# Transposing v on VectorE in 32x32 blocks, with stores to DRAM that put the blocks in place

## The chip, the core and the metric

One core of one Trainium2 chip runs the whole kernel. The metric is device time in microseconds of one execution; the median of several executions is compared between two kernels. The engines are TensorE (PE, its weight loads are shown apart as PEld), VectorE (DVE), ScalarE (ACT), GpSimd (POOL) and SyncE (SP), which issues nearly all transfers. The transfers of SP run on 16 DMA engines that all its transfers share.

## What is computed

Two layers of a small trunk over 640 tokens (128 context tokens and 512 latent ones) of width 1024. Layer A is a chunked gMLP mixer. Layer B is a bidirectional gated DeltaNet with 8 heads, and the change lies in it. Cut to what matters, per head:

```python
proj = h @ w_in                                   # k, q (128 wide), v, z (256 wide) per head
qkv = silu(short_conv(qkv, conv_w))               # 5 taps along the tokens
q, k = l2norm(q) * D_K ** -0.5, l2norm(k)
# gated delta rule, forward and backward over the tokens, state S of 128 x 256:
# S_t = exp(g_t) (I - beta_t k_t k_t^T) S_{t-1} + beta_t k_t v_t^T ;  o_t = S_t^T q_t
o = o_f + flip(o_b)
y = (o * rsqrt(mean(o * o) + eps) * norm_g) * silu(z)
```

The projections leave k, q and v with the channels on the partitions and the tokens along the free dimension. The scan needs v with the tokens on the partitions, so v has to be transposed.

## The kernel before, in words

Layer B is one long software pipeline over the heads. A window `w` is the time of one head: in window `w` the four projections of head `w + 2` are made (`project_head`: k, q and the two halves of v, called q = 0, 1, 2, 3 in the code), the chunk matrices of head `w + 1` (`chunk`), the scan of head `w` (`scan`) and the norm and gate of head `w - 1` (`norm_o`, `gate_z`). `stages()` gives each part a start and an end in units of windows and `PIECES` says into how many pieces its generator is cut; `turns()` sorts all pieces by time. The order of the instructions of PE and SP is the order of these pieces, written down at build time. VectorE, ScalarE and GpSimd get theirs from a scheduler that simulates the program.

After a projection comes `conv` (ScalarE the first tap, L845, VectorE the other four, L848, then Tanh on ScalarE, L851, and `(tanh + 1) * acc` on VectorE, L853). That yields twice the silu, in a buffer `cacc` of 128 channels by 642 columns. For the two halves of v, `post_v` follows (L934): `flip` (L240) transposes the five 128x128 blocks on TensorE into the PSUM tile `px`, of which there is one: four blocks together (tokens 128 to 639), then the first one alone. ScalarE copies each of the two results to the buffer `nat` and halves it there (L938), and one transfer stores `nat` to the DRAM tensor `kvd` of the head (L941). `nat` has one buffer, which k's `post_k` (L905, L907) and both halves of v use in turn. One window later `chunk` loads k from `kvd` (L961), and the scan loads v from it, 128 tokens by 256 columns at a time (`load`, L1097, four buffers). VectorE makes `r` from that v and PSUM (L1115), and TensorE multiplies `r` with the chunk matrices (L1125, L1126).

Of the kernel before, what the change touches and what calls it, by code (L numbers as in the profile page):

```python
# [6 lines left out]
F32 = mybir.dt.float32  # L7
F32R = mybir.dt.float32r
F16 = mybir.dt.float16
AF = mybir.ActivationFunctionType  # L10
# [3 lines left out]
P = 128  # L14
# [9 lines left out]
H = 8  # L24
# [23 lines left out]
NORM_LEN = 1.0  # L48
CONV_AT, CONV_LEN, POST_AT, POST_LEN, NORM_AT, GATE_AT, GATE_STEP = 1.0, 1.0, 2.0, 1.0, 0.4, 1.5, 0.6
CAT, CLEN = 0.0, 0.9  # L50
CSTEP = CLEN / 40 * 4
# [22 lines left out]
def tok(c):  # L74
# [7 lines left out]
PIECES = {"scan": 24, "chunk": 40, "norm_o": 4, "gate_z": 4, "conv": 8, "post_k": 13,  # L82
          "post_q": 7, "post_v": 5, "gates": 7, "gates_e": 26, "residual": 17}


def stages():
# [5 lines left out]
    for w in range(-2, H + 1):  # L92
# [11 lines left out]
        for i, (kind, h, q) in enumerate(slots):  # L104
            i = start + i * wide
            add("project_" + kind, (h, q), i / n, (i + wide) / n, 17)
            if kind == "head":
                i += wide - 1
                add("conv", (h, q), (i + CONV_AT) / n, (i + CONV_AT + CONV_LEN) / n)
                add(("post_k", "post_q", "post_v", "post_v")[q], (h, q), (i + POST_AT) / n,  # L110
                    (i + POST_AT + (KLEN if q == 0 else POST_LEN)) / n)
        if w == -2:
# [95 lines left out]
class Trunk:  # L208
# [421 lines left out]
    def layer_b(self):  # L630
# [4 lines left out]
        self.e_d = self.dram([P, TT, H, P], "ed")  # L635
        self.kv_d = [self.dram([P, TT, P + DV], "kvd") for _ in range(H)]
        with contextlib.ExitStack() as banks, pool("b_c") as bc:
# [11 lines left out]
            self.convw = t(bc, [P, H, 4, CONV], F32, "convw")  # L649
            nc.sync.dma_start(self.convw, a["convw"])  # L650
            self.ngT = t(bc, [P, 2], F32, "ngT")
            nc.sync.dma_start(self.ngT, a["ngT"])
# [185 lines left out]
    def conv(self, h, q):  # L838

        nc, t = self.nc, self.t  # L840
        xp = self.acc[h, q]
        acc = t(self.b2, [P, PADN], F32, "cacc")
        self.acc[h, q] = acc, xp
        w = self.convw[:, h, q]
        nc.scalar.activation(acc, xp[:, 0:PADN], AF.Copy, scale=w[:, 0:1])  # L845
        yield
        for i in range(1, CONV):
            nc.vector.scalar_tensor_tensor(acc, xp[:, i : i + PADN], w[:, i : i + 1], acc, op0=ALU.mult, op1=ALU.add)  # L848
            yield
        th = xp[:, 2 : 2 + PADN]  # L850
        nc.scalar.activation(th, acc, AF.Tanh, scale=0.5)  # L851
        yield
        nc.vector.scalar_tensor_tensor(acc, th, 1.0, acc, op0=ALU.add, op1=ALU.mult)  # L853
        if q != 1:
            self.gap(xp)
        yield
# [29 lines left out]
    def post_k(self, h, q):  # L886
# [7 lines left out]
        for c0 in (1, 0):  # L894
# [11 lines left out]
            yield  # L906
        nc.sync.dma_start(self.kv_d[h][:, :, 0:P], kn)  # L907
        for c0 in (1, 0):
# [22 lines left out]
    def post_v(self, h, q):  # L931
        nc, t = self.nc, self.t
        s, _ = self.acc[h, q]
        v = t(self.b1, [P, TT, P], F32, "nat")  # L934
        for c0 in (1, 0):
            p = self.flip(lambda c: s[:, tok(c)], c0)
            yield
            nc.scalar.mul(v[:, c0 : c0 + p.shape[1], :], p, 0.5)  # L938
            if c0:
                yield  # L940
        nc.sync.dma_start(self.kv_d[h][:, :, P * (q - 1) : P * q], v)  # L941
        yield

    def chunk(self, h, cs):
# [15 lines left out]
        kn = t(b1, [P, nt, P], F32, f"kn{nt}")  # L960
        nc.sync.dma_start(kn, self.kv_d[h][:, those, 0:P])  # L961
        pg = bank()
# [116 lines left out]
    def scan(self, h):  # L1079
# [15 lines left out]
        def load(c):  # L1095
            v = t(b1, [P, DV], F32, "v", bufs=KVB)
            nc.sync.dma_start(v, self.kv_d[h][:, c, P : P + DV])  # L1097
            return v
# [322 lines left out]
```

## Time and profile before

| | |
|---|---|
| median of 3 runs | 1356.4 us (1355.96 to 1357.52) |
| the profiled execution: its time | 1356.03 us |
| the profiled execution: its span | 1354.2 us |
| TensorE busy | 1282.5 us (95%) |
| VectorE busy | 875.7 us (65%) |
| ScalarE busy | 578.7 us (43%) |
| GpSimd busy | 502.0 us (37%) |
| DMA, queue of SP | 157.0 MB, 35.3% of 16 engines' span |

The span runs from the first to the last instruction; the execution's own time is 1.8 us longer. Busy shares are means over stages. Layer B's pipeline runs from about 554 us to 1238 us. Busy time of TensorE counts each matmul from its start to its modelled end, and matmuls overlap.

### The profile page before, as it was taken

Reading aid. Unit: us, or ns where it says so; the run is one execution under the profiler, and the core shown is the slowest. Engines: PE = TensorE matmul, PEld = TensorE weight load, DVE = VectorE, ACT = ScalarE, POOL = GpSimd, SP = SyncE. Lnnn points to the kernel's source line nnn. Section 1 sums busy time; section 2 is a strip of 40 time slices with the busy share of each in tenths; the row PEclk is TensorE's granted clock in tenths of the full one; section 3 lists DMA queues with packets and bytes.
Section 4 is the critical chain, followed back from the end, with each engine's and each line's share of the span. In section 5 each row is a group of like instructions: output and inputs, shape, how many; then the busy total and the mean of one; then the engine's idle time right before and its main releaser. Section 6 shows DMA issues by size and latency. Waiting matters only on the chain. (4 is left out here: it accounts for less than half of the span.)

```text
span 1354.2 us, 22812 instructions
## 1 busy us (share of the span) xinstructions
PE 1282.5 (95%) x8773; PEld 1137.3 (84%) x8773; DVE 875.7 (65%) x1655; ACT 578.7 (43%) x1352; POOL 502.0 (37%) x503
## 2 busy tenths in 40 slices
PE   7999999999999999888999999999999999999996
PEld 4688999999997887778888898999899898887785
DVE  4654744444447566798677778686787868656357
ACT  2333522222224334665545354564545546443320
POOL 0221422222223434354343536355464646520024
PEclk9999999999999999998999999999999999999999
DMA  8512233333336324142122422234233242445732
GB/s 337 168 63 93 94 125 125 125 125 125 125 125 218 118 76 145 56 140 86 50 77 73 136 78 65 100 89 153 79 125 108 85 139 88 133 141 174 261 117 78
DMA packets 90254, 163.17 MB, mean 120 GB/s; under 512 B 9089, under 2 KB 55457, under 8 KB 90017
## 3 DMA queue, kind: packets, MB, share of 16 engines
q1 hardware_dynamic: 88704, 156.99, 35.3%
q10 hardware_dynamic: 1440, 4.72, 1.0%
q8 instruction: 69, 1.13, 0.3%
q14 instruction: 41, 0.33, 0.1%
HBM read 135.97 MB, written 25.71 MB: 119 GB/s over the span
## 5 line engine op out<-in xcount | busy, mean ns | idle before, releaser
L231 POOL TENSOR_TENSOR wlo<-wraw,whi 128x256 fp32r<-128x256 f32 (+1 forms) x188 | 194.4, 1054 | 261.6 <-ACT whi L230 261.6
L235 PE MATMUL pp<-hThi,whi 128*128 128x320 f32 (+1 forms) x784 | 280.1, 357 | 0.2 <-ACT hThi L230 0.2
L237 PE MATMUL pp<-hTlo,whi 128*128 128x320 f32 (+1 forms) x784 | 244.7, 312 | 0.4 <-POOL hTlo L231 0.4
L236 PE MATMUL pp<-hThi,wlo 128*128 128x320 f32 (+1 forms) x784 | 244.1, 311 | 0.0
L230 ACT CAST whi<-wraw 128x256 fp32r<-128x256 f32 (+1 forms) x262 | 143.5, 593 | 84.6 <-PE pacc L236 57.6
L235 PE MATMUL pacc<-hThi,whi 128*128 128x320 f32 x512 | 159.6, 312 | 0.0
L237 PE MATMUL pacc<-hTlo,whi 128*128 128x320 f32 x512 | 158.3, 309 | 0.0
L236 PE MATMUL pacc<-hThi,wlo 128*128 128x320 f32 x512 | 158.2, 309 | 0.0
L848 DVE SCALAR_TENSOR_TENSOR cacc<-xp,convw,cacc 128x642 f32<-128x642 f32 x128 | 137.7, 1076 | 25.0 <-ACT cacc L845 23.6
L235 PEld LDWEIGHTS pp<-hThi,whi 128*128 128x128 f32 (+1 forms) x784 | 148.8, 190 | 3.9 <-ACT hThi L230 0.3
L236 PEld LDWEIGHTS pp<-hThi,wlo 128*128 128x128 f32 (+1 forms) x784 | 148.6, 190 | 4.0
L237 PEld LDWEIGHTS pp<-hTlo,whi 128*128 128x128 f32 (+1 forms) x784 | 147.7, 188 | 1.8 <-POOL hTlo L231 0.7
L231 DVE TENSOR_TENSOR wlo<-wraw,whi 128x1024 fp32r<-128x1024 f32 (+1 forms) x74 | 87.7, 1196 | 60.0 <-ACT whi L230 59.5
L248 POOL TENSOR_TENSOR rs<-ve,mhalf 128x1 f32<-128x1 f32 (+2 forms) x39 | 40.1, 1028 | 170.1 <-DVE ve L246 166.7
L235 PEld LDWEIGHTS pacc<-hThi,whi 128*128 128x128 f32 x512 | 96.1, 188 | 3.1 <-issue 2.2
L236 PEld LDWEIGHTS pacc<-hThi,wlo 128*128 128x128 f32 x512 | 96.1, 188 | 0.0
L237 PEld LDWEIGHTS pacc<-hTlo,whi 128*128 128x128 f32 x512 | 96.1, 188 | 0.0
L256 POOL TENSOR_SCALAR gsq<-gsq 128x320 f32<-128x320 f32 (+1 forms) x52 | 27.7, 532 | 138.4 <-ACT gsq L255 137.4
L257 DVE TENSOR_TENSOR gsq<-pacc,gsq 128x320 f32<-128x320 f32 (+1 forms) x52 | 29.1, 565 | 73.9 <-POOL gsq L256 73.8
L255 ACT ACTIVATE gsq<-pacc 128x320 f32<-128x320 f32 (+1 forms) x52 | 25.7, 498 | 106.2 <-PE pacc L237 102.3
L235 PE MATMUL pacc<-whi,hThi 128*128 128x512 f32 x160 | 63.1, 406 | 7.6 <-ACT whi L230 4.4
L1032 ACT CAST TU<-pt 128x512 f16<-128x512 f32 (+1 forms) x120 | 57.2, 525 | 26.4 <-PE pt L1029 25.5
(333 smaller groups left out, 2974.9 us busy)
## 6 DMA issues: line engine op xcount, KB each, us to landing
wraw<-in_w_b SPq DMA_DIRECT2D x48, 512.0 KB
wraw<-in_w_ada SPq DMA_DIRECT2D x37, 512.0 KB
wraw<-in_w_uz SPq DMA_DIRECT2D x32, 512.0 KB
v<-kvd SPq DMA_DIRECT2D x72, 128.0 KB
wraw<-in_a_wo SPq DMA_DIRECT2D x16, 512.0 KB
wraw<-in_b_wo SPq DMA_DIRECT2D x16, 512.0 KB
kvd<-nat SPq DMA_DIRECT2D x24, 320.0 KB
cacc<-yd SPq DMA_DIRECT2D x24, 320.0 KB
```

Of the source, the lines that this page charges most:

```text
L230: self.nc.scalar.copy(hi, src)
L231: (e_lo or self.nc.vector).tensor_tensor(lo, src, f32(hi), op=ALU.subtract)
L235: mm(out, l_hi, r_hi, start=start, stop=False)
L236: mm(out, l_lo, r_hi, start=False, stop=False)
L237: mm(out, l_hi, r_lo, start=False, stop=stop)
L248: nc.gpsimd.tensor_tensor(r, ve, self.mhalf[:, 0:n], op=ALU.pow)
L255: nc.scalar.activation(sq, u, AF.Square)
L256: nc.gpsimd.tensor_scalar(sq, sq, GB, 1.0, op0=ALU.mult, op1=ALU.add)
L257: nc.vector.tensor_tensor(sq, u, sq, op=ALU.mult)
L848: nc.vector.scalar_tensor_tensor(acc, xp[:, i : i + PADN], w[:, i : i + 1], acc, op0=ALU.mult, op1=ALU.add)
L1032: nc.scalar.copy(part, p.rearrange("p s k t (j b) -> p s (k t j) b", b=b))
```

## The change

v is no longer transposed by TensorE. VectorE transposes `cacc` in blocks of 32x32 (two instructions for each half of v, one of 128x512 and one of 128x128), straight from SBUF to the buffer `nat`. Such an instruction transposes each 32x32 block where it stands. What is left, that block row `b` of channels belongs in column block `b` of the result, is done by four stores, one for each group of 32 partitions, each of 32x20 runs of 32 numbers (128 bytes). For that `kvd` becomes a plain matrix with a row for each token. The halving goes into the weights of v's convolution: they are multiplied by 0.5 once, on GpSimd, and Tanh of v takes its input as it is. Five empty pieces stand between the transposes and the stores, and `post_v` has 7 pieces over 1.4 units in place of 5 over 1.0.

```diff
+VLEN = 1.4
-          "post_q": 7, "post_v": 5, "gates": 7, "gates_e": 26, "residual": 17}
+          "post_q": 7, "post_v": 7, "gates": 7, "gates_e": 26, "residual": 17}
-                    (i + POST_AT + (KLEN if q == 0 else POST_LEN)) / n)
+                    (i + POST_AT + (KLEN, POST_LEN, VLEN, VLEN)[q]) / n)
-        self.kv_d = [self.dram([P, TT, P + DV], "kvd") for _ in range(H)]
+        self.kv_d = [self.dram([NT, P + DV], "kvd") for _ in range(H)]
+            nc.gpsimd.tensor_scalar(self.convw[:, :, 2:4], self.convw[:, :, 2:4], 0.5, 0.0, op0=ALU.mult, op1=ALU.add)
-        nc.scalar.activation(th, acc, AF.Tanh, scale=0.5)
+        nc.scalar.activation(th, acc, AF.Tanh, scale=0.5 if q < 2 else 1.0)
-        nc.sync.dma_start(self.kv_d[h][:, :, 0:P], kn)
+        nc.sync.dma_start(self.kv_d[h].rearrange("(c p) n -> p c n", p=P)[:, :, 0:P], kn)
-        v = t(self.b1, [P, TT, P], F32, "nat")
-        for c0 in (1, 0):
-            p = self.flip(lambda c: s[:, tok(c)], c0)
-            yield
-            nc.scalar.mul(v[:, c0 : c0 + p.shape[1], :], p, 0.5)
-            if c0:
-                yield
-        nc.sync.dma_start(self.kv_d[h][:, :, P * (q - 1) : P * q], v)
+        v = t(self.b1, [P, NT], F32, "nat")
+        nc.vector.transpose(v[:, P:NT], s[:, tok(1).start : tok(4).stop])
+        yield
+        nc.vector.transpose(v[:, 0:P], s[:, tok(0)])
+        for _ in range(5):
+            yield
+        rows = self.kv_d[h].rearrange("(a i) n -> i a n", i=32)
+        for b in range(4):
+            at = P * (q - 1) + 32 * b
+            nc.sync.dma_start(rows[:, :, at : at + 32],
+                              v[32 * b : 32 * b + 32].rearrange("p (a n) -> p a n", n=32))
         yield
-            nc.sync.dma_start(v, self.kv_d[h][:, c, P : P + DV])
+            nc.sync.dma_start(v, self.kv_d[h][c * P : (c + 1) * P, P : P + DV])
```

The loads of k in `chunk` take the same rows from the new layout. Three places where the order moves, all in the window of the fifth head, which stands at 880 to 955 us in the trace of before. The line numbers of the changed kernel are up to 7 higher.

SP, from the end of that head's first half of v to its second half and the loads of v for the scan of the head before (`kvd_4838` is the fifth head's tensor, `kvd_4837` the fourth's; `wraw` is a block of weights, `x` and `rn` belong to the residual, `yd` to the gate). Before:

```order
L961 DMA kn_1803_9808<-kvd_4838 128x2x128
L701 DMA x_80_498<-rn_9675 128x256
L696 DMA rn_9890<-n_76_494 128x256
L941 DMA kvd_4838<-nat_9784 640x1x128
L1215 DMA yd_4821<-z_1502_8471 128x640
L166 DMA wraw_9965<-in_w_b 128x1024
L701 DMA x_81_499<-rn_9890 128x256
L1097 DMA v_10025<-kvd_4837 128x256
L1097 DMA v_10027<-kvd_4837 128x256
```

and now:

```order
L968 DMA kn_1784_9765<-kvd_4838 128x2x128
L704 DMA x_80_498<-rn_9638 128x256
L947 DMA kvd_4838<-nat_9560 32x20x32 x4
L699 DMA rn_9849<-n_76_494 128x256
L1222 DMA yd_4821<-z_1490_8448 128x640
L167 DMA wraw_9922<-in_w_b 128x1024
L704 DMA x_81_499<-rn_9849 128x256
L947 DMA kvd_4838<-nat_9745 32x20x32 x4
L1104 DMA v_9986<-kvd_4837 128x256
L1104 DMA v_9988<-kvd_4837 128x256
```

The second half's one store stood ahead of the gate's store and the weights; its four stores now stand behind them, right ahead of two loads of v. The first half's stores have moved behind the last load of k.

VectorE, where the second half of v is now transposed, and the first use of those loads (L1115, now L1122). Before:

```order
L1213 SCALAR_TENSOR_TENSOR z_1502_8471<-px_9913,ngT_4869,z_1502_8471 128x128
L1134 SCALAR_TENSOR_TENSOR S_9978<-S_9597,scal_4871,ps_9936 128x256
L1140 TENSOR_TENSOR o_9794<-o_9794,ps_9936 128x256
...
L1213 SCALAR_TENSOR_TENSOR z_1552_8666<-px_10012,ngT_4869,z_1552_8666 128x128
L1115 SCALAR_TENSOR_TENSOR r_10079<-ps_10030,neg_4872,v_10025 128x256
L1115 SCALAR_TENSOR_TENSOR r_10082<-ps_10034,neg_4872,v_10027 128x256
L1022 TENSOR_TENSOR Y_1864_10121<-pt_10100,wm_4861 128x2x4x16
```

and now:

```order
L1220 SCALAR_TENSOR_TENSOR z_1490_8448<-px_9872,ngT_4870,z_1490_8448 128x128
L1141 SCALAR_TENSOR_TENSOR S_9935<-S_9562,scal_4872,ps_9893 128x256
L939 STREAM_TRANSPOSE nat_9745<-cacc_9549 128x512
L941 STREAM_TRANSPOSE nat_9745<-cacc_9549 128x128
L1147 TENSOR_TENSOR o_9751<-o_9751,ps_9893 128x256
...
L1220 SCALAR_TENSOR_TENSOR z_1538_8635<-px_9969,ngT_4870,z_1538_8635 128x128
L1029 TENSOR_TENSOR Y_1844_10082<-pt_10061,wm_4861 128x2x4x16
...
L1122 SCALAR_TENSOR_TENSOR r_10040<-ps_9991,neg_4873,v_9986 128x256
L1122 SCALAR_TENSOR_TENSOR r_10043<-ps_9995,neg_4873,v_9988 128x256
```

The two transposes stand between the state update `S` and the output `o`, and the two `r` have moved behind three products `Y` of the chunk part.

VectorE earlier in the same window, at the output `o` of the scan's first unit. Before:

```order
L859 MEMSET xp_766_4887 128x2
L982 SCALAR_TENSOR_TENSOR M_1781_9721<-pe_1779_9714,beta_4873,masks_4857 128x128 x3
L1140 TENSOR_TENSOR o_9603<-o_9603,ps_9696 128x256
L982 SCALAR_TENSOR_TENSOR M_1781_9721<-pe_1779_9714,beta_4873,masks_4857 128x128
L1004 TENSOR_TENSOR TU_1787_9753<-pt_9754,wm_756_4859 128x2x128
```

and now:

```order
L862 MEMSET xp_766_4888 128x2
L989 SCALAR_TENSOR_TENSOR M_1763_9682<-pe_1761_9675,beta_4874,masks_4857 128x128 x2
L1147 TENSOR_TENSOR o_9568<-o_9568,ps_9659 128x256
L989 SCALAR_TENSOR_TENSOR M_1763_9682<-pe_1761_9675,beta_4874,masks_4857 128x128 x2
L1011 TENSOR_TENSOR TU_1769_9714<-pt_9715,wm_756_4859 128x2x128
```

`o` has moved ahead of one of the four masked products `M`.

## Rows read from the trace of the kernel before

**Rows 1.** Page, part 1: busy us (share of the span) and instructions
```profile
PE 1282.5 (95%) x8773; PEld 1137.3 (84%) x8773; DVE 875.7 (65%) x1655; ACT 578.7 (43%) x1352; POOL 502.0 (37%) x503
```

**Rows 2.** Windows: stretch, length, busy PE PEld DVE ACT POOL (x), PEclk, DMA share, GB/s
```profile
554.00:1165.00 611.00, 577.33 (x4498) 533.81 (x4497) 472.94 (x971) 326.59 (x925) 304.06 (x328) 0.99 0.32 99
...
880.00:955.00 75.00, 73.01 (x585) 68.12 (x583) 57.97 (x122) 39.32 (x112) 41.70 (x48) 1.00 0.38 116
...
602.00:609.00 7.00, 4.65 (x31) 4.08 (x29) 7.00 (x13) 1.11 (x3) 4.52 (x5) 1.00 0.38 122
609.00:617.00 8.00, 5.27 (x23) 4.52 (x24) 7.65 (x15) 2.15 (x4) 5.04 (x5) 0.59 0.01 4
```

**Rows 3.** Tiles px and nat: count, duration ns min/median/max, first and last start, forms
```profile
L240 PE MATMUL px<-ident,cacc x120: 270/272/474, 575.3 to 1160.4; 128*128 128x128 f32 x120
...
L938 ACT ACTIVATE nat<-px x32: 257/438/602, 598.6 to 1160.9; 128x512 f32<-128x512 f32 x16, 128x128 f32<-128x128 f32 x16
```

**Rows 4.** Timeline of PE around two flips: start, us, instruction [idle before, releaser]
```profile
913.63 0.31 PE L237 MATMUL pp<-hTlo,whi 128*128 128x320 f32 x1
913.78 0.60 PE L240 MATMUL px<-ident,cacc 128*128 128x128 f32 x4
914.21 1.03 PE L1112 MATMUL ps<-S,kq 128*128 128x256 f32 x4
915.95 1.13 PE L1112 MATMUL ps<-S,kq 128*128 128x256 f32 x4 [0.71 <-DVE o L1140]
...
920.84 0.31 PE L237 MATMUL pp<-hTlo,whi 128*128 128x320 f32 x1
920.99 0.27 PE L240 MATMUL px<-ident,cacc 128*128 128x128 f32 x1
...
921.25 0.31 PE L236 MATMUL pp<-hThi,wlo 128*128 128x320 f32 x1
```

**Rows 5.** Timeline of PE in the first two heads: flips of v that waited, and what followed
```profile
609.13 0.66 PE L240 MATMUL px<-ident,cacc 128*128 128x128 f32 x4 [2.49 <-DVE cacc L853]
...
614.18 0.26 PE L1017 MATMUL pt<-TU,A 128*128 128x64 f16 x2 [2.60 <-DVE TU L1004]
...
679.15 1.11 PE L240 MATMUL px<-ident,cacc 128*128 128x128 f32 x4 [4.44 <-DVE cacc L853]
```

**Rows 6.** Timeline of DVE: idle behind the places where the transposes are put
```profile
898.27 0.69 DVE L1059 TENSOR_TENSOR R<-R,pt 128x512 f16<-128x512 f16 x1 [1.55 <-PE pt L1057]
...
926.00 0.48 DVE L1134 SCALAR_TENSOR_TENSOR S<-S,scal,ps 128x256 f32<-128x256 f32 x1 [1.56 <-PE ps L1126]
```

**Rows 7.** Groups of DVE by form, SBUF to SBUF: count, busy us, mean ns, idle before
```profile
L1052 DVE TENSOR_TENSOR R<-id,T 128x512 f16<-128x512 f16 x16 | 8.6, 538 | 3.7 <-ACT T L1050 3.5
...
L351 DVE TENSOR_TENSOR vh<-vh,y 128x512 f32<-128x512 f32 x8 | 6.9, 878 | 0.0
...
L353 DVE TENSOR_SCALAR vh<-vh,st 128x128 f32<-128x128 f32 x8 | 2.8, 344 | 0.2
```

**Rows 8.** Windows around three transfers that ran alone: kvd store, rn load, abrow load
```profile
843.00:845.50 2.50, 2.50 (x25) 2.40 (x24) 1.63 (x4) 0.00 (x0) 1.66 (x2) 1.00 0.46 131
...
543.50:545.25 1.75, 1.75 (x14) 1.23 (x11) 0.75 (x3) 1.48 (x4) 0.58 (x1) 1.00 0.04 6
918.00:919.50 1.50, 1.50 (x11) 1.45 (x10) 1.35 (x5) 0.75 (x2) 1.39 (x3) 1.00 0.28 87
```

**Rows 9.** Timeline of SP's queue, fifth head: start, us to issue
```profile
910.11 0.54 SPq L941 DMA_DIRECT2D kvd<-nat  x1
...
913.91 0.46 SPq L701 DMA_DIRECT2D x<-rn  x1
...
925.83 0.94 SPq L1097 DMA_DIRECT2D v<-kvd  x2
```

**Rows 10.** Timelines of DVE and PE: where the loaded v is used
```profile
932.40 0.48 DVE L1115 SCALAR_TENSOR_TENSOR r<-ps,neg,v 128x256 f32<-128x256 f32 x1 [0.83 <-PE ps L1112]
...
940.02 0.59 PE L1125 MATMUL ps<-r,G 128*128 128x256 f32 x2
```

More of the change, by code (lines that the diff above doesn't have):

```diff
@@ L960, in chunk @@
         kn = t(b1, [P, nt, P], F32, f"kn{nt}")
-        nc.sync.dma_start(kn, self.kv_d[h][:, those, 0:P])
+        nc.sync.dma_start(kn, self.kv_d[h].rearrange("(c p) n -> p c n", p=P)[:, those, 0:P])
         pg = bank()
```

## The prediction

> **What bounds the kernel now.** The page's first part comes first: TensorE is busy for 95% of the span [rows 1]. That alone does not say what a TensorE instruction is worth, so the stages come next. All that changes lies between 554 and 1165 us, and there TensorE is busy for 577.3 of 611 us, VectorE for 472.9 [rows 2]. In the fifth head's window of 75 us, which the third to seventh heads repeat, it is 73.0 against 58.0 us [rows 2]. So in the middle heads TensorE has about 2 us per window to wait, and what it no longer has to do shortens the window unless another engine is just behind it. The first two heads differ: from 602 to 609 us VectorE is busy for 7.00 of 7.00 us and TensorE for 4.65 [rows 2], and TensorE waits for VectorE at the flips of v, 2.49 and 4.44 us [rows 5]. There VectorE is the bound.
>
> **What the flips cost TensorE.** Each half of v takes five transposes, 16 halves, so 80 of the 120 flips from `cacc`. Their median duration is 272 ns [rows 3], which would make 80 x 0.272 = 21.8 us. But matmuls overlap, so durations don't add up to time on the path; the distance between starts does. A plain matmul takes a step of 0.15 us (913.63 to 913.78, 920.84 to 920.99). Four flips take from 913.78 to 914.21, 0.43 us. One flip and the matmul behind it take from 920.99 to 921.25, 0.26 us, so one flip 0.11 us [rows 4]. A half of v costs 0.54 us, a head 1.08, all eight 8.6 us. That is the most that the removal itself can give, 0.63% of the time, and not 21.8.
>
> **What of it arrives.** In the third to seventh heads I count it in full, 5 x 1.08 = 5.4 us, though one wait stands against that: at 915.95 TensorE waits 0.71 us for VectorE's `o` [rows 4], with both flips of four behind it, so that it would come there some 0.9 us sooner to wait longer. The new order puts `o` ahead of one more `M`, as shown above, and a 128x128 VectorE product is 0.34 us [rows 7]; this and the engine's later idle time are why I take the full figure rather than half. In the first two heads and the last one (3 x 1.08 = 3.2 us) VectorE decides: the wait of 2.49 us is followed by one of 2.60 us for the same engine [rows 5], so an earlier TensorE only waits there longer, and VectorE has more to do. I take 1 us of the 3.2; the bounds are 3.2 us gained and two halves' transposes a head lost, some 6 us by the next part.
>
> **What VectorE gets.** Two transposes a half. No row has one, so the bounds are the nearest operations from SBUF to SBUF: 538 to 878 ns for 128x512, and 344 ns for 128x128 as 2 x 344 at most [rows 7], 0.9 to 1.6 us a half; I take 1.0, since a transpose reads one operand and these read two. Over 16 halves that is 16 us on an engine with 17 us to spare in a window [rows 2]. The places matter more. In the middle heads the first half's transposes stand ahead of an idle stretch of 1.55 us, the second half's behind a state update that itself follows an idle stretch of 1.56 us [rows 6]. So I cost them at nothing there; without that cover it would be up to 3.2 us a window, more than the gain. In the Trainium skill, page "VectorE: DVE Perf Modes", section "The three transpose paths", VectorE's transpose of a 128x128 block (bf16) takes 311 ns; five such blocks would make an estimated 1.6 us a half, the upper end of the range above, and the sum would stay as it is, since this is still about the idle stretch.
>
> **What ScalarE and GpSimd get.** 32 copies of 257 to 602 ns go [rows 3], about 14 us. ScalarE is busy for 39 of 75 us in a window [rows 2]; this is nothing on the path. GpSimd gets one small product before the first convolution, once; the 0.5 of Tanh costs nothing. Both at nothing.
>
> **What the stores cost.** One store of 640 runs of 512 bytes becomes four of 640 runs of 128 bytes. The old one, alone, kept 16 engines busy for 0.46 of 2.5 us, 1.15 us; that is 40 runs on each engine, 29 ns a run [rows 8]. A run of 128 bytes into DRAM is in no row. The `abrow` load has runs of 128 bytes: 0.04 x 1.75 us x 16 = 1.1 us of one engine for the 82 runs that 6 GB/s make in that time, 14 ns a run. The `rn` load's runs of 1024 bytes take 0.28 x 1.5 us over 8 runs on an engine, 52 ns [rows 8]. So a half of v, 160 runs an engine, keeps the engines for 2.2 to 8.3 us. I take 29 ns, the price in the same direction to the same tensor, and so 4.6 us in place of 1.15. SP needs 4 x 0.54 us to issue instead of 0.54 [rows 9].
>
> Who waits for that? First the buffer `nat`: the second half's transposes wait for the first half's stores. These are issued behind the residual's store at 913.91 [rows 9], the last about 2.2 us later, and are done by about 922 even if they start at 916.5; VectorE wants the buffer at 926.48, behind `S` [rows 6]. Covered by 4 us. Second, the two loads of v, issued at 925.83 before [rows 9], now stand behind the second half's stores, so about 4.6 us of transfers and 1.6 us of issuing, partly beside each other, come ahead of them. Before, `r` at 932.40 waited for TensorE and not for the load [rows 10], so v was there by then; now by 937.0 at the latest. TensorE uses `r` at 940.02 [rows 10], two `r` take 0.96 us, so 939.0 would still do, and the order now has three products ahead of `r` that would otherwise wait too. Cover 2 us: at nothing, at the upper end of 8.3 us a delay of 1.7 us a window. The weights issued behind them have three buffers, and k wants `nat` only in the next window.
>
> **The sum.** 5.4 + 1.0 = 6.4 us less, against the profiled execution's own 1356.03 us: 1349.6. The median of the runs is 0.4 us above that execution, which I neglect: 1349.5 us. A measurement of this kernel can tell some 0.2%, 2.7 us, from no change.
>
> **The rivals.**
> *Slow short runs (slower).* If a run under 512 bytes costs DRAM two accesses, a half takes 160 x 58 ns = 9.2 us. v is then there by 941.6 and not by 939.0: 2.6 us of waiting for TensorE in each of six windows with a scan beside a projection, 15.6 us, and the time is 1349.5 + 15.6 = 1365. It decides from (939.0 - 932.4) / 160 = 41 ns a run. For it: no row shows a short run written. Against: 14 ns for a short run read, and less bytes never took longer in these rows. The Trainium skill has this rule ("DMA: Bandwidth & Descriptors", Specifications): below 512 bytes a transfer reads, modifies and writes. By that rule the change would be slower by the sum of this rival; no run here shows it, and the 29 ns of the longer runs leaves it open.
> *VectorE takes it back (no change).* If the waits like the one at 915.95 grow by what TensorE saves, and the transposes delay `Y` and `TU`, a middle window gives 0.1 us and not 1.08, and the first and last heads nothing: 1355.5. For it: 58.0 us of VectorE work in the window becomes 60, and it is continuously busy ahead of that wait. Against: the two idle stretches of 1.55 us [rows 6].
> *The stalls go as well (faster).* The flips of v wait 2.49 and 4.44 us in the first two heads [rows 5]. After the first the granted clock is 0.59 from 609 to 617 us, between its two levels of 1.2 and 2.4 GHz, where it was 1.00 from 602 to 609 [rows 2]; at 5.27 us busy that costs about 2.2 us. If these waits vanish without another in their place, it is 9.1 us more with the full 8.6: 1356.0 - 17.7 = 1338. Against: the wait of 2.60 us right behind, on the same engine.
>
> **How the numbers follow.** My forecast, 1345 to 1353, gets 0.46; some part of the third rival, below 1345, 0.17; no change, 0.20; slower through the short runs, 0.17. So faster by over 0.2% is 0.63, within it 0.20, slower 0.17. The range starts at 1341, which leaves out the better half of the third rival (0.08), and ends at 1361, (1361 - 1349.5) / 6 / 160 = 12 ns above the 41, so a short run of over 53 ns is left out (0.10).
>
> **What would show it.** In the profile of after: no flips from `cacc` but k's 40, no copies to `nat` on ScalarE; 32 transposes of VectorE at 0.9 to 1.6 us a half; TensorE about 71.9 of a window of 74 us; the loads of v landing at most 5 us later and no wait of `r` for a load. The prediction is wrong if `r` or the transposes wait for transfers for more than 1 us a window (short runs), if the windows stay at 75 us with longer waits of TensorE for `o`, `Y` or `TU` (VectorE), or if the first two heads get shorter by more than 3 us.

## The result, and the profile after

The new kernel takes 1368.35 us (median of 6 runs, 1362.97 to 1370.49) against 1356.96 for the kernel before beside it: ratio 1.0077, 95% interval 1.0052 to 1.0101. A second measurement later gave 1.0091 (1.0074 to 1.0109). So it is slower by some 10 to 12 us; the forecast was 1349.5 us and the range ended at 1361. Below, a ratio r is also told as (r - 1) x 1356 us.

The page of after, parts 1 and 3, against [rows 1]:

```profile
PE 1284.0 (94%) x8693; PEld 1136.5 (83%) x8693; DVE 889.5 (65%) x1687; ACT 567.7 (42%) x1320; POOL 508.9 (37%) x504
...
DMA packets 121741, 163.16 MB, mean 119 GB/s; under 512 B 50816, under 2 KB 86944, under 8 KB 121504
...
q1 hardware_dynamic: 120192, 156.99, 35.6%
```

The change did what it says: 80 matmuls and 32 ScalarE copies fewer, 32 VectorE instructions more. Yet TensorE's busy time is not lower than before but 1.5 us higher: matmuls that ran at a lower clock made up for those that are gone. Three stretches of after (length, busy time of PE, PEld, DVE, ACT, POOL, granted clock, DMA share, GB/s):

```profile
554.00:720.00 166.00, 144.22 (x1086) 131.31 (x1086) 135.74 (x268) 90.85 (x258) 70.64 (x62) 0.94 0.27 80
720.00:1155.00 435.00, 417.93 (x3262) 387.90 (x3261) 335.35 (x705) 220.57 (x623) 230.89 (x257) 0.99 0.35 102
1155.00:1260.00 105.00, 92.62 (x605) 78.72 (x604) 64.54 (x146) 39.10 (x96) 29.72 (x35) 0.95 0.44 132
```

and of before:

```profile
554.00:720.00 166.00, 147.47 (x1122) 134.95 (x1121) 134.44 (x263) 94.50 (x268) 70.50 (x62) 0.96 0.27 82
720.00:1155.00 435.00, 421.58 (x3321) 391.81 (x3320) 330.21 (x689) 228.41 (x647) 227.30 (x260) 1.00 0.33 103
1155.00:1260.00 105.00, 98.76 (x652) 83.96 (x651) 63.28 (x139) 42.17 (x98) 26.75 (x32) 1.00 0.51 162
```

In the first two heads and the tail fewer matmuls are done in the same time (1086 for 1122, of which the flips of v are 20; 605 for 652, of which they are 1) at a lower granted clock (0.94 for 0.96, 0.95 for 1.00). The same instruction can be followed through both traces: the first flip of k's first head starts at 583.19 us before and 582.39 after (0.8 ahead), a late flip of the norm at 1169.78 and 1175.08 (5.3 behind), another at 1239.83 and 1252.97 (13.1 behind). So more than half of the loss lies behind 1170 us. The middle windows got hardly shorter: the same product on `Y` recurs after 79.40 us before and 79.09 after (801.50 to 880.90, 803.80 to 882.89); the 75 us of [rows 2] are a part of such a window. Two of the stretches of [rows 2] in after:

```profile
880.00:955.00 75.00, 72.39 (x576) 67.34 (x576) 57.56 (x125) 37.74 (x106) 42.94 (x49) 1.00 0.39 112
...
609.00:617.00 8.00, 3.45 (x14) 3.35 (x14) 8.00 (x17) 2.19 (x5) 4.45 (x5) 0.50 0.11 28
```

The fifth head looks as forecast, TensorE with less to do. But in the first head's stall TensorE now works for 3.45 us where it was 5.27, at a clock of 0.50 for 0.59, while VectorE has not one gap.

What TensorE waits for from 554 to 1275 us (total, times, longest), after:

```profile
PE pt L1024 <- DVE TU L1011: 14.9, 8, 5.6
PE ps L1132 <- ACT o L1125: 6.0, 3, 2.6
PE px L241 <- DVE nat L908: 5.7, 6, 1.4
PE ps L1119 <- issue: 3.5, 1, 3.5
```

and before:

```profile
PE px L240 <- DVE cacc L853: 8.0, 4, 4.4
...
PE pt L1017 <- DVE TU L1004: 4.1, 2, 2.6
...
PE px L240 <- DVE nat L905: 3.4, 3, 1.4
...
PE ps L1125 <- ACT o L1118: 0.9, 1, 0.9
```

The waits of v's flips for `cacc` [rows 5] went with the flips, and longer ones for `TU`, `o` and k's `nat` came. (At the wait marked "issue" the profile names no releaser.) VectorE's new instructions (duration min/median/max):

```profile
L939 DVE STREAM_TRANSPOSE nat<-cacc x16: 697/704/707, 595.5 to 1171.4; 128x512 f32<-128x512 f32 x16
L941 DVE STREAM_TRANSPOSE nat<-cacc x16: 263/270/302, 596.2 to 1172.0; 128x128 f32<-128x128 f32 x16
```

0.97 us a half, as assumed.

### The profile page after: what moved, and what is told of

It reads as the page before. It is cut to its first block, busy times and chain, and to the rows that moved or that the text cites. A ratio compares the mean times of both kernels' runs of the same rounds, so it can differ in the third digit from the quotient of the medians.

```text
span 1367.7 us, 22697 instructions
## 1 busy us (share of the span) xinstructions
PE 1284.0 (94%) x8693; PEld 1136.5 (83%) x8693; DVE 889.5 (65%) x1687; ACT 567.7 (42%) x1320; POOL 508.9 (37%) x504
## 3 DMA queue, kind: packets, MB, share of 16 engines
q8 instruction: 68, 1.11, 0.3%
## 4 chain that ended last, share of the span: by engine, by line
PE 31%; DVE 17%; ACT 5%; DMA 3%; issue 2%; POOL 1%; ACTq 0%; SPq 0%; POOLq 0%; DVEq 0%
PE pp L236 5%; PE pp L238 5%; PE pp L237 5%; DVE cacc L851 5%; PE ps L1119 3%; DVE M L989 3%; PE ps L1133 2%; DMA cacc<-yd 2%; PE ps L1132 1%; ACT junk L879 1%; POOL rs L249 1%; DVE grhs L799 1%; PE pt L1024 1%; DVE cacc L856 1%; DVE A L981 1%
## 5 line engine op out<-in xcount | busy, mean ns | idle before, releaser
L232 POOL TENSOR_TENSOR wlo<-wraw,whi 128x256 fp32r<-128x256 f32 (+1 forms) x188 | 199.1, 1079 | 263.6 <-ACT whi L231 252.5
L1029 DVE TENSOR_TENSOR Y<-pt,wm 128x128 f16<-128x128 f32 (+1 forms) x144 | 47.4, 372 | 37.1 <-PE pt L1024 36.9
```

The costliest lines, as they stand in the source:

```text
L232: (e_lo or self.nc.vector).tensor_tensor(lo, src, f32(hi), op=ALU.subtract)
L1029: nc.vector.tensor_tensor(yc, pair(p), pair(self.wm[:, l - 1, :, 0:nt]), op=ALU.mult)
```

## The experiments

Theories, as they were named: **A**, VectorE's new order (transposes ahead of `TU`, `r` of the last head behind three `Y`); **B**, the short stores; **C**, the transposes ahead of `TU` alone; and, formed after the eighth run, **D**: where VectorE sets the pace, TensorE's saved time comes back as a longer wait with a half clock behind it; **E**, flips cost TensorE their 0.54 us a half everywhere. Ratios are to the kernel before, run beside them.

| run | ratio | 95% | median us |
|---|---|---|---|
| e1 short runs alone | 1.0011 | 0.9998 to 1.0024 | 1357.39 |
| e2 one long store | 1.0029 | 1.0015 to 1.0042 | 1358.97 |
| e3 own buffer for v | 1.0109 | 1.0082 to 1.0136 | 1371.05 |
| e4 stores on GpSimd | 1.0178 | 1.0156 to 1.0201 | 1380.42 |
| e5 stores one yield later | 1.0115 | 1.0094 to 1.0137 | 1370.83 |
| e6 two yields later | 1.0051 | 1.0037 to 1.0066 | 1362.44 |
| e7 before + transposes | 1.0032 | 1.0019 to 1.0045 | 1360.61 |
| e8 no flips, no transposes | 1.0051 | 1.0034 to 1.0068 | 1361.56 |
| e9 e8 + idle flips | 1.0003 | 0.9985 to 1.0020 | 1355.76 |
| e10 e8 in five heads | 0.9978 | 0.9965 to 0.9991 | 1352.77 |
| e11 change in five heads | 1.0014 | 1.0001 to 1.0026 | 1357.42 |
| e12 one half in five heads | 1.0043 | 1.0028 to 1.0059 | 1363.20 |
| e13 e8 in the first two heads | 1.0038 | 1.0022 to 1.0054 | 1359.01 |
| e14 e8 in the last head | 1.0004 | 0.9991 to 1.0017 | 1357.47 |
| e15 new + 30 idle flips | 1.0062 | 1.0045 to 1.0078 | 1363.78 |
| e16 new kernel again | 1.0091 | 1.0074 to 1.0109 | 1370.08 |
| e17 e15 again | 1.0038 | 1.0024 to 1.0052 | 1361.33 |

### Is it the stores? (e1 to e4)

e1, in the kernel before:

```
-        nc.sync.dma_start(self.kv_d[h][:, :, P * (q - 1) : P * q], v)
+        for b in range(4):
+            at = P * (q - 1) + 32 * b
+            nc.sync.dma_start(self.kv_d[h][:, :, at : at + 32], v[:, :, 32 * b : 32 * b + 32])
```

> The kernel before (flips and PSUM copies kept), with v's one store split in four column stores of 128-byte runs; no other engine's order changes. Theory A (the new kernel loses because r and the output step of the last head were placed later in the order, and because VectorE's transposes stand ahead of TU; each new wait of TensorE also lowers its clock): the short runs cost nothing that TensorE sees, 1357 us, plus or minus 2. Theory B (the short runs and the four issues themselves are the loss: 0.55 us more of DMA time per engine and half, and v's loads land later): at least 4 and up to 9 us over the kernel before, 1361 to 1366.

1.5 us, the interval from nothing to 3.3: B's 4 to 9 us are excluded. The short runs alone are not the loss.

e2, in the new kernel, in place of the four stores:

```
+        nc.sync.dma_start(self.kv_d[h].rearrange("(c p) n -> p c n", p=P)[:, :, P * (q - 1) : P * q],
+                          v.rearrange("p (c n) -> p c n", n=P))
```

> The new kernel with the four stores replaced by one of 512-byte runs, so that the 32x32 blocks are not put in place in DRAM (v's values are permuted; all work is otherwise done). The order puts r of the last head back ahead of the three Y, as before the change. Theory A: the tail's wait for ScalarE's o goes (some 5 us with the clock), the waits behind TU in the heads stay: 1360 to 1364. Theory B: the whole loss goes and the flips' gain shows: 1347 to 1352.

3.9 us over before: nearer to A than to B, but below A's range. With long stores alone most of the loss goes, yet no gain shows. Since e1 had put the price of the runs at little, I put what e2 gives back down to the order that the scheduler makes of them; 4.1 us of it can be seen, at the last head's `r` (below, at e5 and e6).

e3 was `"nat"` replaced by `"vt", bufs=2` for v's buffer.

> The new kernel with v's transposed half in buffers of its own (two) in place of those that it shares with k's. The last head's r stays behind the three Y. Theory A: the waits that matter are not for this buffer; 1366 to 1369. Theory B: the stores hold the shared buffer longer and k's normalised product waits for it (TensorE's 0.8 us waits for it, some six of them); with buffers of their own 1361 to 1365.

Slightly above A's range, and B's form of it falls: the shared buffer is not what is waited for (k's flips still wait 5.9 us for `nat`, six times).

e4 was `nc.gpsimd.dma_start` for the four stores.

> The new kernel with the four short stores issued by GpSimd, past SyncE's queue; TensorE's order is that of the new kernel, VectorE's puts r of the last head back ahead of the three Y. Theory A: as with the long store, the tail's wait goes: 1360 to 1364, though each issue takes GpSimd some time. Theory B in the form that the short runs cost DMA time: 1366 to 1370; in the form that SyncE's queue is held up by four issues in place of one: 1352 to 1360.

All expectations missed: 24 us slower, although `r` stood where A wanted it. GpSimd's groups (busy us, mean ns; idle before) and what it waited for ahead of these issues:

```profile
L947 POOL DMA_DIRECT2D kvd<-nat x64 | 45.1, 707 | 38.4 <-DVE nat L941 16.7 <-DVE o L1147 9.8 <-PE pt L1024 8.0
```

64 issues of 707 ns, and 38 us in which GpSimd stood at an issue with the chunk's `A`, `L` and `TU` queued behind it; TensorE's longest wait for `TU` grew to 7.4 us. On SP, which computes nothing here, the same 64 issues stand ahead of other transfers alone.

### Is it VectorE's order and time? (e5 to e7)

e5 and e6 put one and two yields more ahead of the stores (`VLEN` 1.6 and 1.8, 8 and 9 pieces); TensorE's order stays that of the new kernel.

> The new kernel with each half's stores one yield later (VLEN 1.6, eight pieces): the second half's four stores are issued behind the scan's loads of v instead of ahead of them. TensorE's order stays, VectorE's puts r of the last five heads back ahead of the three Y; the transposes keep their place ahead of TU. Theory A (order): the tail's wait for ScalarE's o goes, TU's waits stay: 1359 to 1363. Theory C (only the transposes ahead of TU cost, the tail's wait is worth nothing): 1366 to 1369. Theory B (short stores): 1364 to 1369.

> The new kernel with two yields more in each half (VLEN 1.8, nine pieces): stores behind the loads of v, and the second half's transposes of the last five heads behind the third TU instead of ahead of it; TensorE's order stays. Theory A: the tail's wait and the 0.8 us waits behind TU go, the wait at 613 us of the first head stays: 1352 to 1359. Theory C: 1360 to 1364. Theory B: 1364 to 1369.

In both the last head's `r` is early again. What that is worth shows in the trace of after. There VectorE has `r` behind `Y`:

```profile
1180.10 0.95 DVE L1029 TENSOR_TENSOR Y<-pt,wm 128x128 f16<-128x128 f32 x3 [3.95 <-PE pt L1024]
...
1182.17 0.87 DVE L1122 SCALAR_TENSOR_TENSOR r<-ps,neg,v 128x256 f32<-128x256 f32 x2
```

ScalarE then has `o` behind a cast of weights:

```profile
1182.83 1.35 ACT L231 CAST whi<-wraw 128x256 fp32r<-128x256 f32 x4
1184.06 0.87 ACT L1125 ACTIVATE o<-ps,scal 128x256 f32<-128x256 f32 x2
```

and TensorE waits:

```profile
1184.61 0.70 PE L1132 MATMUL ps<-r,G 128*128 128x256 f32 x2 [2.26 <-ACT o L1125]
```

Followed instruction by instruction, after loses 4.1 us on before between 1175 and 1185 us; e5 and e6 lose nothing there. e6 came out at 6.9 us over before, above A's range and in C's: the 0.83 us waits for `TU` in the middle heads stayed. (They are not the transposes' doing: e10, below, has no transposes and has these waits.) e5 missed them all: it won the 4.1 us back in the tail and lost more in the middle. GpSimd in e5:

```profile
952.39 0.73 POOL L701 TENSOR_TENSOR rn<-rn,lnb 128x256 f32<-128x256 f32 x1 [5.32 <-DMA rn<-n]
...
958.80 0.74 POOL L701 TENSOR_TENSOR rn<-rn,lnb 128x256 f32<-128x256 f32 x1 [3.58 <-DMA rn<-n]
...
961.67 1.02 POOL L249 TENSOR_TENSOR rs<-ve,mhalf 128x4 f32<-128x4 f32 x1
```

VectorE in e5:

```profile
962.73 0.69 DVE L908 TENSOR_TENSOR nat<-px,rs 128x512 f32<-128x512 f32 x1 [4.97 <-POOL rs L249]
```

The residual's `rn` lands late, GpSimd stands at it, and VectorE waits 4.97 us for k's `rs`, which is behind it in GpSimd's order (0.91 us in before and after); TensorE waits 3.3 us for k's `nat`. A load that nobody on the path needs stopped the engine that the path needs next.

e7, in the kernel before, ahead of v's flips:

```
+        x = t(self.b1, [P, NT], F32, "vt", bufs=2)
+        nc.vector.transpose(x[:, P:NT], s[:, tok(1).start : tok(4).stop])
+        nc.vector.transpose(x[:, 0:P], s[:, tok(0)])
```

> The kernel before, all of it kept, with the two VectorE transposes of each half added into a buffer that nothing reads (16 times 0.97 us on VectorE, ahead of the first TU of each head): VectorE's price without any gain. Theory A: TensorE waits some 0.8 us a head more behind TU, each wait with a lower clock behind it: 1362 to 1368. Theory B (VectorE's time lies in its idle stretches, the stores are the loss): 1356 to 1359.

4.3 us for 15.5 us of VectorE work, between the two ranges: VectorE's time is not free, but it is not the whole loss either.

### Is there a gain at all? (e8 to e10)

e8, in the new kernel: no transposes, `s` stored as it stands.

```
-        nc.vector.transpose(v[:, P:NT], s[:, tok(1).start : tok(4).stop])
-        nc.vector.transpose(v[:, 0:P], s[:, tok(0)])
...
+        nc.sync.dma_start(rows[:, 1:TT, at : at + P],
+                          s[:, tok(1).start : tok(4).stop].rearrange("p (c n) -> p c n", n=P))
+        nc.sync.dma_start(rows[:, 0, at : at + P], s[:, tok(0)])
```

> The new kernel without VectorE's transposes: v is stored as it stands in its projection, channel by channel, in two stores of 512-byte runs a half, so v's values stand in the wrong places; flips and PSUM copies are gone as in the new kernel. This is the gain without the price. If TensorE's time was worth what the forecast took (8.6 us less): 1346 to 1350. If the flips lay in time that TensorE would wait through anyway: 1354 to 1358. Theory B has no say in it, the runs are long.

Every expectation missed, and this decided the case. 80 matmuls and 32 copies taken away, nothing put in their place, and the program is 6.9 us slower. Here is why, in the second head. TensorE before, from the flip that waited 4.44 us [rows 5] on:

```profile
680.86 2.53 PE L1112 MATMUL ps<-S,kq 128*128 128x256 f32 x8
683.41 0.22 PE L1017 MATMUL pt<-TU,A 128*128 128x64 f16 x2
683.48 1.10 PE L964 MATMUL pt<-kq 128*128 128x256 f32 x4
```

and in e8, which was 2.8 us behind on arriving here, 2.3 of them already at 550 us, ahead of all that the change touches:

```profile
677.75 1.03 PE L1116 MATMUL ps<-S,kq 128*128 128x256 f32 x4
682.30 1.10 PE L1116 MATMUL ps<-S,kq 128*128 128x256 f32 x4 [3.52 <-issue]
686.19 0.26 PE L1021 MATMUL pt<-TU,A 128*128 128x64 f16 x2 [2.78 <-DVE TU L1008]
686.26 2.05 PE L968 MATMUL pt<-kq 128*128 128x256 f32 x4
```

VectorE before and then in e8, at the same place:

```profile
680.30 2.73 DVE L982 SCALAR_TENSOR_TENSOR M<-pe,beta,masks 128x128 f32<-128x128 f32 x3
682.95 0.41 DVE L1004 TENSOR_TENSOR TU<-pt,wm 128x256 f16<-128x256 f32 x1
```

```profile
683.07 2.73 DVE L986 SCALAR_TENSOR_TENSOR M<-pe,beta,masks 128x128 f32<-128x128 f32 x3
685.72 0.41 DVE L1008 TENSOR_TENSOR TU<-pt,wm 128x256 f16<-128x256 f32 x1
```

`TU` ends a stretch in which VectorE has no gap; it comes 2.77 us later in e8, exactly by what e8 was behind. The flips changed nothing about when TensorE may go on: before, they and `ps` filled the time until `TU`, and TensorE did not wait for it. Without them it waits, first 3.52 us (VectorE's `o` ends at 682.20, just ahead), then 2.78 us for `TU`, and then its four products take 2.05 us in place of 1.10: the granted clock from 686 to 690 us is 0.50, its lower level of 1.2 GHz, where before it is 1.00 from 684 to 688. Before, the clock fell too, behind the wait of 4.44 us: four flips took 1.11 us [rows 5] in place of 0.60 [rows 4]. But what ran slowly then was work that `TU` covered. So the removed work comes back as waiting, and the waiting costs the clock on top: e8, 2.8 us behind at 676, is 4.6 behind at 690.

e9 puts the 80 flips back, into PSUM that nothing reads:

```
+        for c0 in (1, 0):
+            self.flip(lambda c: s[:, tok(c)], c0)
+            yield
...
```

With them `post_v` goes back to 5 pieces over 1.0 unit, so that the stores stand earlier too.

> The run without transposes (v stored channel by channel, so its values stand in the wrong places), with TensorE's flips put back where they stood before, into PSUM that nothing reads: TensorE's and VectorE's orders are those of the kernel before, only ScalarE's 32 copies are missing. Theory D (the flips lay in time in which TensorE waits for VectorE's chain, in the first two heads and the last, and filling that time keeps its clock up): adding these 80 matmuls makes the program faster than the run without them, 1354 to 1358. Theory E (the flips cost TensorE what the forecast took, and the run without them lost its time to something else): 1366 to 1371.

1.0003: with 80 matmuls *added* (and earlier stores) the program is 6 us faster. D is what was seen, E is excluded; that the flips alone do it, e15 and e17 have to show, where nothing else is changed. And since ScalarE's copies are the only work on an engine that e9 lacks against before, they are worth nothing that can be measured here (the interval ends 2.7 us above before).

e10 takes e8's edit only where TensorE sets the pace (`if 2 <= h <= 6`).

> Flips and PSUM copies kept in the first two heads and the last, gone from the five heads between, where v is stored channel by channel without transposes (values in the wrong places there). Theory D: TensorE sets the pace in these five heads, by the trace of the run without any transposes some 0.7 us a head come through, and the losses of the first and last heads do not arise: 1350 to 1353. Theory E, or if the gain depends on nothing but the number of flips: 5/8 of that run's loss, 1358 to 1361.

3.0 us less (1.2 to 4.7): here removed flips do give time, 0.6 us a head of the 1.08. The rest goes into waits. TensorE in the fifth head:

```profile
914.07 1.13 PE L1129 MATMUL ps<-S,kq 128*128 128x256 f32 x4 [0.48 <-DVE o L1157]
...
916.47 0.22 PE L1034 MATMUL pt<-TU,A 128*128 128x64 f16 x2 [0.83 <-DVE TU L1021]
```

Before, it waited there 0.71 us for `o` [rows 4] and not at all for `TU`; now it is 1.31 us for both, 0.60 more, and 1.08 - 0.60 = 0.48 us are left.

### Where it arises, and the change itself in part (e11 to e17)

e11 does the whole change (with e6's yields) in the five middle heads and keeps the flips in the other three; e12 does it there for the second half of v alone.

> All of the computation done: flips in the first two heads and the last, VectorE's 32x32 blocks with their short stores (two yields later than in the new kernel) in the five heads between. Theory D: the losses of the first and last heads are gone, and in the middle VectorE's part takes back the 0.7 us a head: 1354 to 1358. If VectorE's place and the short stores cost in every head alike (theories A and B): 1360 to 1363.

> As the run before it, but only the second half of v goes through VectorE's blocks in the five middle heads, the first half keeps its flips; apart from the added transposes VectorE's order is that of the kernel before. Theory D: half the gain and half the price of the middle heads, 1353 to 1357. Theories A and B: 1358 to 1360.

e11 is as D expected and the best version that does all of the computation, but no faster than before. Against e10, VectorE's blocks with their stores cost 1.9 + 3.0 = 4.9 us in five heads. One way that the traces show: GpSimd's `rn` products have moved under VectorE's convolution. VectorE in e11, then in e10:

```profile
952.00 2.71 DVE L853 SCALAR_TENSOR_TENSOR cacc<-xp,convw,cacc 128x642 f32<-128x642 f32 x2 [1.69 <-ACT cacc L850]
954.63 0.75 DVE L1061 COPY U<-TU 128x256 f16<-128x256 f16 x1
```

```profile
951.75 1.81 DVE L853 SCALAR_TENSOR_TENSOR cacc<-xp,convw,cacc 128x642 f32<-128x642 f32 x2 [1.70 <-ACT cacc L850]
953.48 0.22 DVE L1058 COPY U<-TU 128x256 f16<-128x256 f16 x1
```

In e11 GpSimd is busy from 952.0 to 954.0 and again from 954.5; in e10 it is idle from 951.8 to 954.3. The convolution's two steps and the copy take 1.4 us longer beside GpSimd's products; k's `nat` comes 6.51 us behind the convolution's start in place of 5.62, and TensorE waits 0.84 us for it, in three of the heads; e10 has no such wait. That is about half of the 4.9; the rest was not followed.

e12 missed every expectation, with 5.8 us. Its waits from 720 to 1155 us:

```profile
PE ps L1132 <- DVE o L1160: 6.2, 5, 1.6
```

Before has 3.9 us there in five. VectorE, then TensorE in the fifth head:

```profile
917.68 0.41 DVE L1160 TENSOR_TENSOR o<-o,ps 128x256 f32<-128x256 f32 x1
...
918.85 0.70 DVE L942 STREAM_TRANSPOSE nat<-cacc 128x512 f32<-128x512 f32 x1
```

```profile
918.14 1.13 PE L1132 MATMUL ps<-S,kq 128*128 128x256 f32 x4 [1.16 <-DVE o L1160]
```

The transposes stand behind this `o`, so they do not delay it. TensorE waits 1.16 us for it in place of 0.71 because the four flips ahead of it, 0.43 us [rows 4], are gone: they came back whole as waiting. The transposes then stand ahead of `TU` (0.4 us of waiting a head, 1.9 in all), and k's `nat` is waited for as in e11 (2.5 us in three heads). Less of the change is not less of its price; the 5.8 us were not followed to the end.

e13 and e14 take e8's edit to the first two heads (`if h < 2`) and to the last (`if h == 7`).

> The kernel before, with v of the first two heads alone stored channel by channel (values in the wrong places there), without flips, PSUM copies or transposes; VectorE's order is otherwise that of the kernel before. Theory D: VectorE sets the pace there and TensorE's saved time comes back as a longer wait with a half clock behind it: slower than the kernel before by 2 to 5 us, 1357.5 to 1361. Rival: the loss of the run without any transposes is all in the last head: 1353 to 1356.

> The same for the last head alone: its flips, copies and transposes gone, all else as before; VectorE's order is that of the kernel before. Theory D: by the trace of the run without any transposes the stretch from 1155 us on loses 4 to 5 us, so 1358 to 1361. Rival: the tail's loss there came from v's loads landing late by chance or from the other heads' changes: 1354 to 1357.

The first two heads alone lose 5.1 us (3.0 to 7.3); the last alone loses nothing that can be measured, against D's expectation. Its trace does have the longer wait: at 1152.89 us TensorE waits 2.80 us for `TU` where before it was 1.45. In e13, behind the first head's stall:

```profile
612.00:616.00 4.00, 0.00 (x0) 0.00 (x0) 4.00 (x5) 0.00 (x0) 3.92 (x4) 0.59 0.28 82
616.00:620.00 4.00, 3.05 (x13) 2.96 (x13) 3.42 (x11) 1.79 (x4) 1.13 (x2) 0.50 0.09 25
```

TensorE does nothing for 4 us, then works at half clock. VectorE, without a gap in the first 4, sets the end.

e15 and e17 are the new kernel with the flips of the first two heads and the last put back unread; e16 is the new kernel, beside e17.

> The new kernel, all of its computation done, with 30 of the removed flips put back in the first two heads and the last, into PSUM that nothing reads: work added to TensorE and nothing taken away. Theory D: it gets faster than the new kernel's 1368.4, 1361 to 1366. Rival (TensorE sets the pace, every matmul costs its time: 0.54 us a half, six halves): 1370 to 1373.

> The new kernel unchanged, on the same chip and in the same rounds as the next run, because the interval of its first measurement (1.0052 to 1.0101 of the kernel before) overlaps that of the run with idle flips (1.0045 to 1.0078). Theory D: ratio 1.008 to 1.010, slower than the run with idle flips by 0.2 to 0.4%. Rival (the idle flips give nothing): both the same within 0.1%.

> The run with 30 idle flips in the first two heads and the last, again, beside the new kernel. Theory D: ratio 1.005 to 1.006. Rival: the new kernel's ratio or up to 0.25% above it.

1.0038 (to 1.0052) against 1.0091 (from 1.0074): 30 idle matmuls make the new kernel 7 us faster. e17 came out even below its expectation. The first pair, after and e15, is 2 us apart with overlapping intervals, so the size is somewhere from 2 to 7 us. That it is the waits can be read from the traces; what was 14.9 us for `TU` in after is in e17

```profile
PE pt L1028 <- DVE TU L1015: 7.1, 7, 1.6
```

The rival that the flips only moved VectorE's order falls too: the last head's `r` still comes late in e15 and e17, with the same 4.1 us lost there.

### Where the traces put the loss

Leaving out the flips, TensorE's products stand in the same order in nearly all of these kernels, so each can be looked up in two traces. How many us a run falls behind before, by stretches of before's trace (minus: it catches up):

| run | to 550 us | 550 to 720 | 720 to 1135 | 1135 to 1262 |
|---|---|---|---|---|
| after | -0.8 | 2.8 | 1.6 | 10.5 |
| e16, the same kernel | -0.4 | 0.7 | -0.1 | 9.7 |
| e17, with idle flips | -0.6 | -0.1 | -0.5 | 6.7 |
| e6 | 2.3 | 2.7 | 0.3 | 4.3 |
| e8 | 2.3 | 2.3 | -3.5 | 5.4 |
| e13, first two heads | 2.8 | 2.6 | -2.6 | 0.6 |
| e14, last head | -1.7 | -0.8 | -2.4 | 1.7 |

All kernels do the same work up to 550 us, and e14 does what before does up to 1135 (but for the halving, which went into the weights), so a stretch of one trace can be off by 2 to 3 us through the execution alone. One source can be seen: a fall of TensorE's clock that one trace has and another has not. First a place where before has one (granted clock 0.57), behind a wait of 0.83 us, and e14 has none (1.00) behind 0.78; then the same products of the last head in before and in after, behind equal waits (0.39 and 1.25 us, 0.39 and 1.24):

```profile
1054.00:1058.00 4.00, 4.00 (x18) 3.74 (x16) 1.53 (x4) 0.58 (x1) 2.12 (x3) 0.57 0.03 10
1209.00:1213.00 4.00, 4.00 (x19) 3.49 (x20) 2.71 (x3) 2.24 (x6) 3.51 (x3) 1.00 0.46 138
```

```profile
1219.00:1223.00 4.00, 4.00 (x13) 3.28 (x12) 2.47 (x3) 1.17 (x3) 3.27 (x3) 0.61 0.52 165
```

The first costs 1.6 us in before and in five of the 18 other traces, and nothing in the rest; the second costs 1.7 us in ten of the 18, after, e6, e16 and e17 among them, and nothing in the rest. What decides it is open.

Even so the table shows that the new kernel loses most in the last head and behind it: 4.1 us at `r`; 1.4 to 1.6 from 1135 to 1175 us, which the idle flips take away (0.2 in e17); 1.7 by that fall of the clock; and in after 1.7 where VectorE's `r` waits for its load. Before, then after:

```profile
1217.06 0.98 DVE L1115 SCALAR_TENSOR_TENSOR r<-ps,neg,v 128x256 f32<-128x256 f32 x2 [1.03 <-DMA v<-kvd]
```

```profile
1230.20 0.88 DVE L1122 SCALAR_TENSOR_TENSOR r<-ps,neg,v 128x256 f32<-128x256 f32 x2 [2.73 <-DMA v<-kvd]
```

## Why the prediction was wrong

**The step that failed** is "What of it arrives". I counted 5.4 us for the five middle heads and took 1 us of 3.2 from the first two and the last, arguing that there "an earlier TensorE only waits there longer". That sentence was right and its price was wrong: I took the longer wait as free. It is not, since TensorE comes out of it at half clock (0.50 in e8 and e13). In place of 1.0 us gained, the first two heads cost 5.1 by the medians (e13, 3.0 to 7.3) and 2.3 to 2.8 by the traces of after, e6, e8 and e13 (0.7 in e16); in e13's trace another 2.8 us were lost ahead of 550 us, where nothing was changed. My bound of 6 us lost held that, but for VectorE's extra work, and e13 has none. In place of 5.4, the five heads give 3.0 (e10). There I had counted on `o` moving ahead of one `M` to spare a wait; it does (0.71 us becomes 0.32 in after's fifth head), but TensorE then waits 0.83 us for `TU`, which VectorE finishes no sooner.

**VectorE at nothing** failed too. The size was right (0.97 us a half against 1.0), the cover was not: the transposes cost 4.3 us alone (e7), where one half's stand ahead of `TU` in the middle heads, and 4.9 us in five heads together with the stores (e11 against e10).

**The reordered `r`** I read as favourable ("three products ahead of `r` that would otherwise wait too"). In the last head it is the opposite: 4.1 us lost at 1184 us. **The loads of v** I took as covered, with no wait of `r` for one; in the last head `r` waited 1.03 us for its load already before, and 2.73 in after. Short runs are not what it takes: in e8, with long ones, it is 2.54.

**The stores** were overpriced. From after's and before's share of the busiest queue, (0.356 x 1367.7 - 0.353 x 1354.2) = 8.9 us of each engine over 16 halves, 0.55 us a half: with the old store's 1.15 some 1.7 us for 160 runs, 11 ns a run. In e1 the same sum (36.5% of 1356.1) gives 2.2 us, 14 ns. The traces also time each packet: the 128-byte ones took 13.4 ns on the mean in after and 13.8 in e1, those of 512 bytes 28.8 in before, so a half takes about 2.1 us, a little under my lower bound of 2.2, and not 4.6. The rival of slow short runs named 1365, near the truth, by a mechanism that is not there: it needed 58 ns a run. That rival rested also on the Trainium skill, page "DMA: Bandwidth & Descriptors", section Specifications (below 512 bytes a transfer reads, modifies and writes); the measured 13.4 ns a run show no doubling, and the measurement decides.

**ScalarE at nothing** was right, as far as e9 can tell. Of the other rivals, *VectorE takes it back* was right about VectorE (4 to 5 us), but there was no gain of 6 us to take back, and *the stalls go as well* was the very opposite: the stalls stayed and grew.

**The sum as the runs have it**: 5.1 (first two heads, e13) + 1.9 (five heads with blocks and stores, e11) + 0.5 (last head, e14) = 7.5 us, where e6, which has all these, shows 6.9. `r` behind `Y` adds 4.1 by the trace: 11.0 for the new kernel, measured 10.4 and 12.3. That the sum closes so well is in part luck: the first three terms are each uncertain by some 2 us, and the traces give the first two heads less than 5.1 and the last head more than 0.5.

**Open.** e13, e10 and e14 add up to 2.6 us where e8 shows 6.9 (4.6 to 9.2); by the traces the rest of e8's loss lies behind 1135 us, where TensorE waits 2.80 us for `TU` and 2.46 for an `o` whose `v` landed late; why that load is late in some versions was not settled, nor why the clock falls there in some. Why e2 with its transposes is no slower than e8 without (the intervals overlap) is open as well.

## What to carry to other kernels

Before work is taken off the busiest engine, ask stretch by stretch whether that engine sets the pace there; where another does, the work is filling, and without it the wait is longer and TensorE's next products may run at half clock. Try the gain without its price first (e8: leave the work out and put nothing in its place), and put it back without readers to see whether its time counts (e9, e17). Follow the same instructions through two traces before a stretch is blamed, and see first how far two executions differ where nothing was changed. An edit in a scheduled program is priced with its order: the short stores cost 1.5 us as transfers (e1), and the order that came with them 4.1 us at one place in the last head.

## What was not expected of the hardware

Idle matmuls can speed a program up: 30 of them by 0.5% (e17 against e16; 0.15%, not clear of noise, for e15 against after), 80 together with earlier stores by 0.5% (e9 against e8). TensorE's clock fell to half for some 4 us behind waits of equal length in one trace and not in another, at 1.6 to 1.7 us each time. VectorE transposes 128x512 f32 in 32x32 blocks in 704 ns and 128x128 in 270. The issue of a short store took 707 ns on GpSimd (mean, e4) and 606 on SP (mean, after; median 520). A VectorE copy of 128x256 f16 took 0.22 us with GpSimd idle and up to 0.75 beside its products. A run of 128 bytes took a DMA engine 13.4 ns, one of 512 bytes 28.8.
